# A planned kernel on one core: DMAs put in the program's order, and the planner's durations remade

## The chip, the cores and the metric

The kernel runs on one core of a Trainium2 chip. The core has a matrix engine (TensorE, PE in the profile), a vector engine (VectorE, DVE), a scalar engine (ScalarE, ACT), GpSimd (POOL), and SyncE (SP), which here issues every DMA; 16 DMA engines carry out the transfers. Each engine takes its instructions in a fixed order from a queue of its own and waits at a semaphore where an operand is not there yet. The metric is the device time of one execution in microseconds (us). The kernel before takes 1733.99 us, the median of three runs (1732.49 to 1739.18).

## The reference

One inference step of a trunk of two layers, on a prompt of 1024 tokens and 8 samples of 4 tokens, with D_MODEL = 1024, all in float32. Each layer computes `x + gate(c) * Branch(RMSNorm(x) * (1 + scale(c)) + shift(c))`. Layer 0 is attention in a sliding window of 128 with a sink for each head; layer 1 is a gated DeltaNet with 16 value heads in 8 groups. Its core, cut to what matters:

```python
lower = where(strict, einsum('nbhik,nbhjk->nbhij', kb, kc) * decay, 0.0)
sol = triangular_solve(lower + eye(chunk), rhs, lower=True, unit_diagonal=True)
w_v, w_k = sol[..., :dv], sol[..., dv:]
def step(S, xs):
    u = w_v_c - einsum('bhck,bhkv->bhcv', w_k_c, S)
    o = einsum('bhck,bhkv->bhcv', q_dec_c, S) + einsum('bhij,bhjv->bhiv', qk_c, u)
    S = S * g_tot_c + einsum('bhck,bhcv->bhkv', k_dec_c, u)
    return S, o
out = (rms_norm(o, o_norm_g) * silu(z)) @ w_out
```

The outputs are the rows of the prompt and the samples after a last norm, the new caches of keys and values, the convolution states, and the DeltaNet states of prompt and samples. The states of the samples are 8 x 16 matrices of 128 x 128, 8 MB read and 8 MB written.

## The kernel before

A product in float32 is made of three matmuls: both operands are split into a high part and a rest (`wh` and `wl`, `h2hi` and `h2lo`), and high·high, rest·high and high·rest are summed. The prompt is cut into 8 blocks of 128 tokens; a projection takes one 128-column tile of weights against all 1056 rows in three groups of 384, 384 and 288 columns (`project`, `ps_pj`). These projection matmuls are the filler: everything else is put between them.

Who comes when is decided while the program is written. `Engine` wraps each engine of the core, so that every instruction goes through `Core.issued`. It keeps a clock for each engine (`free`), and for each tile when it was last written and used (`written`, `used`); it adds the duration of the instruction from a small table and links it to the one before on its engine with an edge "program order". Work beside the projections is written as generators that `weave` puts in a list of jobs by rank (`K`, `KR`). After each projection matmul `stages` lets each job go on as long as its condition holds: `ready`, `soon` and `idle` compare the planner's clocks with TensorE's, `bank` waits for a free PSUM bank, `until` runs the jobs until something has come about. So the durations decide how many projection matmuls are laid between, say, a product and the instruction that needs its result. Every recorded instruction has line L89 in the profile (the wrapper's call).

DMA issues were not linked before: they have a place by their data dependences, and the library's scheduler put them into SP's queue.

The parts that the texts below speak of:
- `solve(hq)` makes the products of the keys of head group `hq` (`cst,kT` are transposes, `kT,kT` the products) and scales them into `UZ`; `invert(hq)` inverts 64 triangular 32x32 blocks at once in 31 steps on VectorE, each a product into `tmp` and a subtraction from `X`, 62 rows in all; `diagonal` and `blocks` put these into the whole inverse (`Xd,UZ` products, a transpose of `Xd` into `UZ` on VectorE, `UZ,M` products).
- `decayed(hq)` scales the `qT,kT` products into `DP` on VectorE, `chain(hq)` is the recurrence over 8 chunks. Ahead of the key projection of the group after next the program waits until the chain is finished (`until(lambda: finished[0] >= r - 1)`), so the end of `chain(0)` has no projections beside it.
- The convolution (`conv`) of each projection tile runs as nine `qT`, `kT` or `vT` rows on VectorE (three taps for each of three column groups).
- `out_block(b)` is the output projection of block `b`: it loads `of<-gTd`, adds to the row block `xt<-x2d` and stores `out_y_p<-xt`, with two buffers of `xt`. Beside it `new_states` renews the samples' states: it loads a unit into a buffer (`S<-in_state_gdn_s`), scales it and adds a product (`U,kb`), and stores it (`out_new_s_s<-S`); there are three buffers, and each turn of its loop first fetches the unit two ahead and at its end stores its own. From some point on a unit is 8 heads, 512 KB.

Of the kernel before, what the change touches and what calls it, by code (L numbers as in the profile page):

```python
# [5 lines left out]
F32 = mybir.dt.float32  # L6
# [71 lines left out]

class Engine:
# [16 lines left out]
class Core:  # L96


    def __init__(self, tc):
        self.tc, self.nc = tc, tc.nc  # L100
        self.free, self.last = {}, {}
        self.written, self.used, self.slots, self.parts, self.wide = {}, {}, {}, set(), {}
        self.group = 0
# [7 lines left out]
    def issued(self, eng, op, ins, args, kwargs):  # L111
        aps = [a for a in (*args, *kwargs.values()) if hasattr(a, "tensor")]
        outs = [a for a in (kwargs.get("out", aps[0]), kwargs.get("accum_out")) if a is not None]
        srcs = [a for a in aps if not any(a is o for o in outs)]
        n = 1
        for d in outs[0].shape[1:]:
            n *= d
        start = self.free[eng]
        for a in srcs:
            start = max(start, self.after(self.written, a, eng))  # L120
            if a.space == PSUM:
                start = max(start, self.after(self.used, a, eng))
        for a in outs:
            if self.used.get(self.key(a), (0.0, ""))[1] != "sync" or eng != "sync":
                start = max(start, self.after(self.used, a, eng))
        if "dma" in op:
            self.free[eng] = start + 0.45
            end = start + 2.4
        else:
            rate, fixed = {"tensor": (2400 if op == "matmul" and srcs[0].dtype == F32R  # L130
                                      else 1200 if op == "transpose" else 600, 0.004),
                           "scalar": (1200, 0.06 if op == "copy" and srcs[0].space == PSUM else 0.14
                                      if srcs and srcs[0].space == PSUM else 0.18),
                           "vector": (960, 0.13 if op == "scalar_tensor_tensor" else 0.08),
                           "gpsimd": (420, 0.02 if n >= 256 else 0.14)}[eng]
            if op == "matmul" and outs[0].shape[0] <= 64 and srcs[0].dtype == F32:
                rate = 2400 if n <= 64 and outs[0].shape[0] <= 32 else 600 * P / outs[0].shape[0] if self.group != outs[0].offset // outs[0].ap[0][0] else rate
            if eng == "tensor":
                self.group = outs[0].offset // outs[0].ap[0][0]
            if op == "tensor_scalar_mul" and srcs and srcs[0].space != PSUM and eng == "vector":  # L140
                rate = 1920
            if op == "memset":
                rate = 1e9
            end = self.free[eng] = start + fixed + n / rate
            if eng in self.last:
                self.tc.add_manual_dep(ins, self.last[eng],
                                       mybir.DependencyInfo(mybir.DependencyClass.NoSync, mybir.DependencyReason.DATA),
                                       reason="program order")
            self.last[eng] = ins.name
        for a in srcs:  # L150
            self.used[self.key(a)] = max(self.used.get(self.key(a), (0.0, "")), (end, eng))
        for a in outs:
            self.written[self.key(a)] = self.used[self.key(a)] = (end, eng)

    def key(self, a):

        if a.tensor.name in self.wide:
            return a.tensor.name, a.offset % a.ap[0][0] // self.wide[a.tensor.name]
        return (a.tensor.name, a.offset) if a.tensor.name in self.parts else a.tensor.name

    def after(self, table, a, eng):
        t, e = table.get(self.key(a), (0.0, eng))
        return t + (0.0 if e == eng == "tensor" else 0.1 if e == eng else 0.2)

    def slot(self, key, bufs, t):
# [3 lines left out]
        if len(q) > bufs:  # L169
            self.used[q[-1]] = self.used.get(q[-1 - bufs], (0.0, ""))  # L170
# [7 lines left out]
class Watched:  # L178
# [3 lines left out]
    def tile(self, shape, dt, tag=None, name=None, bufs=None):  # L182
# [5 lines left out]
        self.core.used.setdefault(t.tensor.name, (self.since, "pool"))  # L188
# [31 lines left out]
def body(tc, I, O, cst_ap, dbg=None):  # L220
# [316 lines left out]
    def bank(tag):  # L537
# [5 lines left out]
        yield lambda: plain() or nc.after(nc.used, t, "tensor") <= nc.free["tensor"]  # L543
# [220 lines left out]
    if True:  # L764
# [38 lines left out]
        def kproj(pr):  # L803
# [10 lines left out]
            def evac(gi, a0, b0, pj):  # L814
                if pr == 1 and gi == 0:
                    until(lambda: begun[0] >= 2 * NB)
                    zo[1] = zp.tile([P, 4, T], F32, tag="zo1", name="zo")
                    nc.parts.add(zo[1].tensor.name)
# [217 lines left out]
        def cached():  # L1036

            nonlocal sa_guard, sa
            yield lambda: attended[0] == 4 * NB
# [134 lines left out]
        def open_wo(n):  # L1174
# [3 lines left out]
            for w, nm in ((whi, "whi"), (wlo, "wlo")):  # L1178
                t_ = wo.tile([P, n, D], F32R, name=nm)
                nc.parts.add(t_.tensor.name)  # L1180
# [110 lines left out]
        nc.parts.add(zo[0].tensor.name)  # L1291
# [21 lines left out]
    if True:  # L1313
# [10 lines left out]
        nc.parts.add(x1d.tensor.name)  # L1324
# [320 lines left out]
    if True:  # L1645
# [7 lines left out]
        for XR in XRs:  # L1653
            nc.wide[XR.tensor.name] = GW
            nc.gpsimd.memset(XR[:, 0:3], 0.0)
# [449 lines left out]
        def place_out(k0, wh_, wl_):  # L2105

            nc.parts |= {wh_.tensor.name, wl_.tensor.name}
# [85 lines left out]
        nc.parts |= {x2d.tensor.name, gTd.tensor.name}  # L2193
# [525 lines left out]
```

## Time and profile before

| | |
|---|---|
| median of three runs | 1733.99 us |
| profiled execution | 1732.34 us |
| span of its instructions | 1730.6 us |
| PE busy | 1621.2 us, 94%, 10666 matmuls |
| DVE busy | 1174.6 us, 68%, 3538 |
| ACT busy | 862.6 us, 50%, 2514 |
| POOL busy | 675.5 us, 39%, 1576 |
| mean granted clock of TensorE | 0.98 |
| DMA | 191.82 MB, 111 GB/s over the span |

The profile is of one execution. A row of a timeline gives the start and the length of an instruction (or of a run of like ones, with their count), its engine and line, output and inputs, and in brackets how long the engine stood idle before it and what it waited for. A row of the view of waits gives the engine and its output, what it waited for, the total, the number and the longest. A row of the view of windows gives a stretch of time and the busy time of each engine in it, then the granted clock, the share of DMA time and the rate in GB/s. SPq is SP's queue of DMA issues. The ends of matmuls are modelled: rows of one engine may overlap, and the distance from start to start is the time that one takes.

### The profile page before, as it was taken

The page shows a single profiled execution, that of the slowest core. Times are in us where ns is not written, and L with a number is a line of the kernel's source. Part 1 is how long each engine was busy: PE and PEld are TensorE (multiplying, and loading weights), DVE is VectorE, ACT ScalarE, POOL GpSimd, SP SyncE. Part 2 cuts the span into 40 slices and gives each one's busy share as a digit, 9 for nine tenths or more (in the row PEclk, how much of TensorE's full clock was granted, in tenths as well). Part 3 has the DMA queues.
Part 4 walks back from the last instruction along what each step waited for, and adds up shares of the span by engine and source line. Part 5 has one row for each costly group of instructions (what it writes and reads, how often), then busy time and mean ns, then how long its engine had stood idle before and what let it go on. Part 6 is the DMA issues. An engine that isn't in the chain of part 4 may idle for free. (4 is left out here: it accounts for less than half of the span.)

```text
span 1730.6 us, 32224 instructions
## 1 busy us (share of the span) xinstructions
PE 1621.2 (94%) x10666; PEld 1429.5 (83%) x10666; DVE 1174.6 (68%) x3538; ACT 862.6 (50%) x2514; POOL 675.5 (39%) x1576
## 2 busy tenths in 40 slices
PE   6999999999999999589999999999999998989897
PEld 5987888977788889469989999899999996657675
DVE  4426675555565787757878778778697776357676
ACT  5625555453335664166554655554655655332332
POOL 2601121122213356235544654546356565323332
PEclk9999999999999999799999999999999999999998
DMA  9542122234233323122412324224132237764885
GB/s 330 153 133 73 51 58 55 51 103 114 92 122 97 105 55 85 29 68 69 127 42 73 102 58 114 65 69 117 46 104 70 56 93 227 218 190 138 244 268 171
DMA packets 281577, 191.82 MB, mean 111 GB/s; under 512 B 98361, under 2 KB 253881, under 8 KB 281378
## 3 DMA queue, kind: packets, MB, share of 16 engines
q1 hardware_dynamic: 281410, 189.75, 38.2%
q8 instruction: 85, 1.39, 0.3%
q14 instruction: 82, 0.67, 0.1%
HBM read 144.68 MB, written 47.04 MB: 111 GB/s over the span
## 5 line engine op out<-in xcount | busy, mean ns | idle before, releaser
L89 POOL TENSOR_TENSOR wl<-wr,wh 128x128 fp32r<-128x128 f32 x488 | 236.7, 515 | 485.5 <-ACT wh L89 449.4
L89 PE MATMUL ps_pj<-h2hi,wh 128*128 128x384 f32 (+1 forms) x1128 | 379.9, 337 | 0.0
L89 PE MATMUL ps_pj<-h2lo,wh 128*128 128x384 f32 (+1 forms) x1128 | 378.1, 335 | 0.0
L89 PE MATMUL ps_pj<-h2hi,wl 128*128 128x384 f32 (+1 forms) x1128 | 376.8, 334 | 0.0
L89 PEld LDWEIGHTS ps_pj<-h2hi,wh 128*128 128x128 f32 x1128 | 213.2, 189 | 3.1 <-ACT wh L89 0.2
L89 PEld LDWEIGHTS ps_pj<-h2hi,wl 128*128 128x128 f32 x1128 | 213.2, 189 | 2.7 <-POOL wl L89 0.2
L89 PEld LDWEIGHTS ps_pj<-h2lo,wh 128*128 128x128 f32 x1128 | 213.0, 189 | 2.2
L89 POOL TENSOR_TENSOR xt<-xt,y 128x512 f32<-128x512 f32 (+1 forms) x48 | 63.6, 1328 | 194.3 <-DVE y L89 170.4
L89 PE MATMUL ps_pj<-hlo,wh 128*128 128x384 f32 (+1 forms) x360 | 119.1, 331 | 0.0
L89 PE MATMUL ps_pj<-hhi,wh 128*128 128x384 f32 (+1 forms) x360 | 118.4, 329 | 0.0
L89 PE MATMUL ps_pj<-hhi,wl 128*128 128x384 f32 (+1 forms) x360 | 118.1, 328 | 0.0
L89 DVE SCALAR_TENSOR_TENSOR vT<-XR,cT,vT 128x384 f32<-128x384 f32 (+1 forms) x144 | 83.9, 591 | 47.4 <-ACT vT L89 45.3
L89 DVE TENSOR_TENSOR tmp<-X 64x31 f32<-64x31 f32 (+15 forms) x248 | 89.0, 359 | 16.9 <-POOL X L89 13.4
L89 DVE TENSOR_TENSOR X<-X,tmp 64x31 f32<-64x31 f32 (+15 forms) x248 | 90.7, 366 | 8.5
L89 ACT CAST wh<-wr 128x512 fp32r<-128x512 f32 x122 | 75.1, 617 | 16.4 <-PE ps_pj L89 11.3
L89 POOL TENSOR_TENSOR Xd<-Xc,cst 32x128 f32<-32x128 f32 x128 | 62.7, 490 | 40.5 <-DVE UZ L89 24.4
L89 PEld LDWEIGHTS ps_pj<-hlo,wh 128*128 128x128 f32 x360 | 67.7, 188 | 10.5 <-issue 10.5
L89 ACT COPY XR<-ps_pj 128x384 f32<-128x384 f32 (+1 forms) x96 | 43.0, 448 | 59.5 <-PE ps_pj L89 59.4
L89 PEld LDWEIGHTS ps_pj<-hhi,wh 128*128 128x128 f32 x360 | 67.7, 188 | 4.0 <-issue 3.1
L89 ACT ACTIVATE prob<-prob,nm 128x256 f32<-128x256 f32 (+1 forms) x128 | 62.2, 489 | 15.5 <-DVE nm L89 15.3
L89 PEld LDWEIGHTS ps_pj<-hhi,wl 128*128 128x128 f32 x360 | 67.7, 188 | 2.2 <-issue 2.1
L89 ACT ACTIVATE qe<-ps_mi,Eg 128x128 f32<-128x128 f32 x112 | 34.9, 363 | 60.4 <-PE ps_mi L89 60.3
(574 smaller groups left out, 4203.9 us busy)
## 6 DMA issues: line engine op xcount, KB each, us to landing
wr<-in_gdn_w_in SPq DMA_DIRECT2D x96, 256.0 KB
S<-in_state_gdn_s SPq DMA_DIRECT2D x40, 256.0 KB
xt<-in_x_prompt SPq DMA_DIRECT2D x16, 512.0 KB
wm<-in_w_mod SPq DMA_DIRECT2D x16, 512.0 KB
wr<-in_swa_w_in SPq DMA_DIRECT2D x64, 128.0 KB
wmod<-in_w_mod SPq DMA_DIRECT2D x32, 256.0 KB
wm<-in_w_mod SPq DMA_DIRECT2D x32, 256.0 KB
DP<-gcr SPq DMA_DIRECT2D x64, 128.0 KB
```

The source lines that it names most:

```text
L89: inst = fn(*args, **kwargs)
```

## The change

Five things change, all in the planner. (1) The edge "program order" is added behind every instruction, DMA issues included, so that SP's queue has the order in which the program wrote them. (2) Durations are taken by engine, operation, shape and operands (`on_tensor`, `on_scalar`, `on_vector`, `on_gpsimd`), with TensorE at half speed for 4 us after a gap of more than 2.2 us, table loads on ScalarE, waits between VectorE and GpSimd for a shared port, and a queue of transfers. (3) Tiles are tracked by the box of rows and columns that an access touches (`box`, `note`, `over`) in place of the whole tile or of a listed part (`parts`, `wide`). (4) The latencies between engines are new (`after`), and the time at which a buffer is free comes from `freed`, which leaves out uses by the same engine. (5) `bank` asks `freed`, and the stage `cached` also waits until the stage `modulate` is over. The ranks and all that is computed stay.

```diff
@@ Core.issued
-            if self.used.get(self.key(a), (0.0, ""))[1] != "sync" or eng != "sync":
-                start = max(start, self.after(self.used, a, eng))
+            start = max(start, self.freed(a, eng))
         if "dma" in op:
-            self.free[eng] = start + 0.45
-            end = start + 2.4
+            self.free[eng] = start + 0.48
+            onto = outs[0].space != DRAM
+            size = outs[0].shape[0] * n if onto else int(np.prod(outs[0].shape))
+            part = min(4 * self.run(outs[0]), 4 * self.run(srcs[0]), 4096)
+            work = size * 4 / part * (8.5 + part * 0.0375) * 7e-5
+            self.queue = max(self.queue, start + 0.9) + work
+            few = (outs[0] if onto else srcs[0]).shape[0] <= 64 and part >= 2048
+            end = done = max(start + 2.0, self.queue + 1.0 + work * (1.5 if few else 0.5))
         else:
-            rate, fixed = {"tensor": (2400 if op == "matmul" and srcs[0].dtype == F32R
...
-            end = self.free[eng] = start + fixed + n / rate
-            if eng in self.last:
-                self.tc.add_manual_dep(ins, self.last[eng],
...
+            start, dur, late = getattr(self, "on_" + eng)(op, start, base, n, outs, srcs, args, kwargs)
+            self.free[eng], end, done = start + dur, start + dur + late, start + dur + 0.02
+        if eng in self.last:
+            self.tc.add_manual_dep(ins, self.last[eng],
...
     def after(self, table, a, eng):
-        t, e = table.get(self.key(a), (0.0, eng))
-        return t + (0.0 if e == eng == "tensor" else 0.1 if e == eng else 0.2)
+        lag = {"tensor": 0.054, "gpsimd": 0.078}.get(eng, 0.036)
+        return max((t + (0.06 if e == "sync" else 0.02 if e == eng else lag) for t, e in self.over(table, a)
+                    if not e == eng == "tensor"), default=0.0)
+
+    def freed(self, a, eng):
+        lag = {"tensor": 0.054, "gpsimd": 0.078}.get(eng, 0.036)
+        return max((t + lag for t, e in self.over(self.used, a, a.space == PSUM) if e != eng), default=0.0)
+
+    def on_tensor(self, op, start, base, n, outs, srcs, args, kwargs):
+        if start - base > 2.2:
+            self.slow = 4.0
+        rows = outs[0].shape[0]
+        tiled = rows <= 64 and srcs[0].dtype == F32 and op == "matmul"
...
+        elif srcs[0].dtype == F32R:
+            dur = max(0.108, n / 2400 + 0.014)
+        else:
+            dur = (1 if op == "transpose" else 2) * max(0.108, n / 1200 + 0.003)
...
@@ bank
-        yield lambda: plain() or nc.after(nc.used, t, "tensor") <= nc.free["tensor"]
+        yield lambda: plain() or nc.freed(t, "tensor") <= nc.free["tensor"]
@@ cached
-            yield lambda: attended[0] == 4 * NB
+            yield lambda: attended[0] == 4 * NB and over("modulate")()
```

Where this moves instructions: first VectorE's queue at the end of the inverse of head group 0 and the start of that of group 1 (`X` and `tmp` are rows of the inverse, `qT` rows are convolution taps, `DP` rows scale the products of `decayed`, and the transpose puts a diagonal block into `UZ`). Before:

```order
L89 SCALAR_TENSOR_TENSOR qT<-XR_6117,cT,qT 128x256
L89 TENSOR_TENSOR tmp<-X 64x60
L89 TENSOR_TENSOR X<-X,tmp 64x2x30
L89 SCALAR_TENSOR_TENSOR qT<-XR_6117,cT,qT 128x256
L89 TENSOR_TENSOR tmp<-X 64x31
L89 TENSOR_TENSOR X<-X,tmp 64x31
L89 TENSOR_SCALAR epq<-gsq 128x8
L89 SCALAR_TENSOR_TENSOR DP<-ps_lg,sj,DP 128x128 x14
L89 TENSOR_TENSOR tmp<-X 64x31
L89 TENSOR_TENSOR X<-X,tmp 64x31
L89 STREAM_TRANSPOSE UZ<-Xd_6600 128x512
```

And of the change:

```order
L92 TENSOR_TENSOR tmp<-X 64x31
L92 TENSOR_TENSOR X<-X,tmp 64x31
L92 SCALAR_TENSOR_TENSOR qT<-XR_6141,cT,qT 128x384 x3
L92 SCALAR_TENSOR_TENSOR qT<-XR_6141,cT,qT 128x256 x3
L92 TENSOR_SCALAR epq<-gsq 128x8
L92 SCALAR_TENSOR_TENSOR DP<-ps_lg,sj,DP 128x128 x7
L92 STREAM_TRANSPOSE UZ<-Xd_6579 128x512
L92 SCALAR_TENSOR_TENSOR DP<-ps_lg,sj,DP 128x128
L92 COPY UZ<-ps_lg 32x4x32
L92 SCALAR_TENSOR_TENSOR DP<-ps_lg,sj,DP 128x128 x3
L92 TENSOR_TENSOR tmp<-X 64x31
L92 TENSOR_TENSOR X<-X,tmp 64x31
```

The inverse of group 0 ends ahead of six of the nine `qT` rows in place of behind all of them, and the first transpose stands ahead of the inverse of group 1, in place of behind its first step. The second transpose comes behind all 62 rows of that inverse in both, here with five more `DP` rows ahead of it:

```order
L92 TENSOR_TENSOR tmp<-X 64x31
L92 TENSOR_TENSOR X<-X,tmp 64x31
L92 SCALAR_TENSOR_TENSOR DP<-ps_lg,sj,DP 128x128 x5
L92 STREAM_TRANSPOSE UZ<-Xd_6581 128x512
L92 STREAM_TRANSPOSE UZ<-Xd_6579 128x512
```

On TensorE, between the first `Xd,UZ` products and the `UZ,M` products of 64 columns that need the second transpose, there are 59 projection matmuls before (35 of 384 columns and 24 of 288) and 111 in the change (63 and 48), with a group of `qT,kT`. The change has its first rows of that place so:

```order
L92 MATMUL ps_lg<-Xd_6579,UZ 128x96 x4
L92 MATMUL ps_pj<-h2hi,wh 128x384
L92 MATMUL ps_pj<-h2lo,wh 128x384
L92 MATMUL ps_pj<-h2hi,wl 128x384
L92 MATMUL ps_pj<-h2hi,wh 128x384
L92 MATMUL ps_pj<-h2lo,wh 128x384
L92 MATMUL ps_lg<-UZ,M 32x32 x4
L92 MATMUL ps_lg<-qT,kT 128x128 x4
```

Before, `UZ,M` of 32 columns came 60 rows behind the first `Xd,UZ`, right behind the second group of them; the `qT,kT` products lay ahead of both.

Then SP's queue in the last stage (`S` are state buffers, the number is that of the tile). Before:

```order
L89 DMA out_new_s_s<-S_19891 128x8x128
L89 DMA out_y_p<-xt 128x1024
L89 DMA S_20034<-in_state_gdn_s 128x8x128
L89 DMA out_new_s_s<-S_19918 128x8x128
L89 DMA xt<-x2d 128x1024
L89 DMA of<-gTd 128x4x128
L89 DMA S_20098<-in_state_gdn_s 128x8x128
L89 DMA of<-gTd 128x4x128
L89 DMA out_y_p<-xt 128x1024
L89 DMA out_new_s_s<-S_19940 128x8x128
```

And of the change:

```order
L92 DMA out_new_s_s<-S_19890 128x8x128
L92 DMA S_20078<-in_state_gdn_s 128x8x128
L92 DMA of<-gTd 128x4x128
L92 DMA out_new_s_s<-S_19947 128x8x128
L92 DMA S_20127<-in_state_gdn_s 128x8x128
L92 DMA out_y_p<-xt 128x1024
L92 DMA xt<-x2d 128x1024
L92 DMA of<-gTd 128x4x128
L92 DMA out_new_s_s<-S_20035 128x8x128
L92 DMA S_20221<-in_state_gdn_s 128x8x128
L92 DMA of<-gTd 128x4x128
```

A store and the load into the buffer that it empties stand next to each other in the change, nine times for `S` and five for `xt` between the first state load of 512 KB and the last state store; before, another issue stands between them in most cases.

More of the change, by code (lines that the diff above doesn't have):

```diff
@@ new lines, in on_vector @@
+    def on_vector(self, op, start, base, n, outs, srcs, args, kwargs):
+        scaled = op.startswith("tensor_scalar")
+        rate = 1920 if scaled and (not srcs or srcs[0].space != PSUM) else 960
+        fixed = 0.075
+        if op == "scalar_tensor_tensor":
+            fixed = 0.128 if n > 32 else 0.09
+        elif scaled and len(srcs) > 1:
+            fixed = 0.13
+        elif op == "transpose":
+            fixed = 0.1
+        dur = 0.0 if op == "memset" else fixed + n / rate
+        big = sum(a.space != PSUM and np.prod(a.shape[1:]) >= max(2, n // 2) for a in srcs)
+        if big > 1 or big and rate == 1920:
+            for x, y in reversed(self.pool[-12:]):
+                if x <= start < y:
+                    start = y
+            self.port.append((start, start + dur))
+        return start, dur, 0.08
```

138 lines of the change are left out of this document (97 added, 41 removed).

## The prediction

> **What bounds the kernel now.** I read the windows first, one per stage: start; attention layer; projections and first head group of the DeltaNet layer; its first recurrence, `chain(0)`; the seven later head groups; the output projection with the sample states; and the end of that.
>
> ```profile
> core 0: us, PE busy (x) PEld busy (x) DVE busy (x) ACT busy (x) POOL busy (x), PEclk, DMA share, GB/s
> 0.00:43.00 43.00, 28.98 (x215) 23.20 (x216) 20.86 (x77) 21.79 (x36) 10.50 (x22) 0.96 0.98 331
> 43.00:389.00 346.00, 338.76 (x2367) 296.24 (x2367) 193.99 (x696) 183.46 (x563) 81.68 (x152) 1.00 0.30 84
> 389.00:692.00 303.00, 290.82 (x1814) 254.72 (x1812) 196.19 (x579) 143.49 (x363) 110.89 (x222) 0.99 0.34 96
> 692.00:779.00 87.00, 60.21 (x460) 48.99 (x461) 59.53 (x164) 32.94 (x105) 26.47 (x86) 0.86 0.20 49
> 779.00:1428.00 649.00, 634.97 (x4444) 603.74 (x4444) 511.89 (x1467) 377.12 (x1199) 345.32 (x970) 1.00 0.30 80
> 1428.00:1600.00 172.00, 156.27 (x877) 115.55 (x877) 101.04 (x266) 63.35 (x158) 62.96 (x99) 0.96 0.65 193
> 1600.00:1731.00 131.00, 111.16 (x497) 87.09 (x494) 91.09 (x293) 40.44 (x93) 37.70 (x29) 0.95 0.75 228
> ```
>
> The rows sum to PE 1621 busy of 1731. Length less PE busy gives the idle time: 14.0, 7.2, 12.2, 26.8, 14.0, 15.7 and 19.8, together 109.8 us. TensorE is the bound, and its work stays: the change can only move idle time and the clock. VectorE comes near it only in `chain(0)` (59.5 against 60.2). So I read what ended the idle time, and where the last matmul stands.
>
> ```profile
> PE ps_lg L89 <- DVE UZ L89: 19.0, 6, 16.9
> PE ps_pj L652 <- DVE dg L640: 11.7, 2, 9.8
> PE ps_mi L89 <- ACT kb L89: 6.8, 4, 3.3
> PE ps_tr L89 <- ACT vT L89: 5.6, 5, 2.3
> PE ps_lg L89 <- DMA S<-in_state_gdn_s: 5.3, 3, 2.3
> PE ps_lg L89 <- DVE KQT L89: 4.4, 1, 4.4
> ...
> PE ps_lg L89 <- ACT kT L89: 3.6, 2, 3.3
> ...
> 1717.84 0.39 PE L89 MATMUL ps_ob<-h2lo,ohi 128*128 128x512 f32 x1
> ```
>
> (Total us, times, longest.) Of the 109.8, the 14.0 at the start (most of it the 11.7 behind `dg`) stand in an order that the change leaves alone, and 1730.6 − 1718.2 = 12.4 is the tail behind the last matmul: 109.8 − 14.0 − 12.4 = **83 us** are open to the change. One wait is large, 16.9; the rest are many of 1 to 4 us.
>
> **The change, part by part.** Nothing is computed differently: no term for added or removed work. The sum goes by stage against the profiled execution, 1732.34 us (span 1730.6), which is 1.65 below the median of 1733.99.
>
> *The long wait in `chain(0)`.*
>
> ```profile
> 678.79 1.03 PE L89 MATMUL ps_lg<-Xd,UZ 128*128 128x96 f32 x8
> ...
> 689.05 1.03 PE L89 MATMUL ps_lg<-Xd,UZ 128*128 128x96 f32 x8
> 690.65 0.44 PE L89 MATMUL ps_lg<-UZ,M 128*32 128x32 f32 x8 [0.58 <-ACT M L89]
> 708.01 1.06 PE L89 MATMUL ps_lg<-UZ,M 128*32 128x64 f32 x16 [16.92 <-DVE UZ L89]
> ...
> 680.86 0.18 DVE L89 TENSOR_TENSOR tmp<-X 64x31 f32<-64x31 f32 x1 [2.00 <-POOL X L89]
> ...
> 681.20 0.69 DVE L89 STREAM_TRANSPOSE UZ<-Xd 128x512 f32<-128x512 f32 x1
> ...
> 706.42 0.60 DVE L89 SCALAR_TENSOR_TENSOR DP<-ps_lg,sj,DP 128x128 f32<-128x128 f32 x2
> 706.94 0.69 DVE L89 STREAM_TRANSPOSE UZ<-Xd 128x512 f32<-128x512 f32 x1
> ```
>
> VectorE takes the second transpose of `UZ` only behind the whole triangular inverse of the next head group (680.86 to 706.4, 25.6 us). In the changed order the second transpose still stands behind all 62 rows of that inverse: the wait stays. What changes is TensorE's cover. Between the first `Xd,UZ` and the waiting `UZ,M` (of 64 columns) TensorE now has 59 projection matmuls (35 of 384 columns, 24 of 288), which fill 679.8 to 689.05: 9.2 us, 0.157 each. Changed it has 111 (63 and 48): 111 × 0.157 = 17.4, and four `qT,kT` products, about 1 like the group of `Xd,UZ`: 9 us more cover. Against it, seven more `DP` rows of 0.3 and a small copy stand between the two transposes, 2.3 us. So 16.9 − 9.2 + 2.3 = 10 remain: **−7**. Bounds: −16.9 (all covered) to +2.3 (the cover then lacks elsewhere in `chain(0)`, which has no projections of its own). That the inverse of the first group starts and ends earlier in the new order is how the cover grows (the first diagonal product comes earlier in TensorE's row); it is not counted again.
>
> After long waits the clock is lower. Behind those of 3.27 and 16.92 us:
>
> ```profile
> 628.56 0.47 PE L89 MATMUL ps_lg<-cst,kT 128*128 128x128 f32 x1 [3.27 <-ACT kT L89]
> ...
> 709.00:715.00 6.00, 5.49 (x42) 4.73 (x42) 2.67 (x6) 0.49 (x1) 2.43 (x6) 0.50 0.28 44
> 628.00:634.00 6.00, 5.44 (x31) 5.44 (x32) 5.57 (x14) 5.01 (x18) 0.98 (x2) 0.72 0.03 5
> ```
>
> Of the six microseconds behind each, 6 × 0.28 = 1.7 and 6 × 0.50 = 3.0 are lost. The first is counted with the small waits; the second stays as long as ten microseconds of its wait do.
>
> *The small waits, 43 to 692.* 7.2 + 12.2 = 19.4 idle, and 1.7 of clock. The planner thought an operand ready there and it wasn't (`kT`, `vT`). With durations and latencies nearer to the traces a matmul is put later, behind filler that exists here in plenty (TensorE is at 0.97). Bounds: all gone, with the clock, −21; or a third more of them, +7, since another order makes new ones. Nearest is what is left in the best stage, 43 to 389, which idles at 2.1%; 389 to 692 at that rate would keep 6.4 of its 12.2 and lose 5.8: **−6**.
>
> *779 to 1428:* 14.0 idle in 649, already 2.2%. By the same bounds −14 to +5; I take **−4**, most of what `vT` makes. *1428 to 1600:* 15.7, with 4.4 behind `KQT` and 5.3 behind state loads, which are true chains; the rest is 6: **−4**, bounds −10 to +5.
>
> *The end, 1600 on.* Here transfers decide. SP issues every DMA in one row, and an issue that waits holds all behind it.
>
> ```profile
> SPq L89 <- DMA out_new_s_s<-S: 31.9, 12, 7.0
> SPq L89 <- DMA out_y_p<-xt: 20.1, 6, 5.9
> ...
> 1653.22 0.57 SPq L89 DMA_DIRECT2D out_new_s_s<-S  x1
> 1660.04 0.37 SPq L89 DMA_DIRECT2D S<-in_state_gdn_s  x1
> ...
> 1712.96 0.34 SPq L89 DMA_DIRECT2D out_y_p<-xt  x1
> 1716.20 0.33 SPq L89 DMA_DIRECT2D xt<-x2d  x1
> ...
> 1700.37 0.39 PE L89 MATMUL ps_pj<-whB,ohi 128*64 128x512 f32 x1
> 1700.60 0.28 PE L89 MATMUL ps_mi<-U,kb 96*128 96x256 f32 x1
> 1700.72 0.39 PE L89 MATMUL ps_pj<-wlB,ohi 128*64 128x512 f32 x1
> ```
>
> A load into a buffer that was just stored waits for the store to land: 3.24 us with the queue free (1712.96 to 1716.20), 6.8 under load (1653.22 to 1660.04). The new order has each such load right behind its store: 9 pairs of state buffers and 5 of `xt` from the first 512 KB state load to the last state store. The planner's new `freed` skips users on the same engine, so it thinks these 14 waits free. At w us each, and some 13 us for about 30 issues of 0.33 to 0.57, the row takes 14w + 13: 58 us at 3.2, 76 at 4.5, 108 at 6.8. In the same stretch TensorE has (rows of the changed order, 221 matmuls of 512 columns at 0.23, start to start, and 48 state products at 0.12) 57 us, and 128 such matmuls, 29 us, behind the last state product. With only one or two transfers in flight at a time I expect the landing nearer to 3.2 than to 6.8: w = 4.5, so SP is 76 − 57 = 19 late, of which the 29 us behind cover about 10 (they need `of` tiles from the same queue): **+9**. Bounds: −7 (the 6.8 behind `kb` goes, nothing new) to +35.
>
> A rule speaks against this order. The Trainium skill, page "DMA: Bandwidth & Descriptors", section "Anatomy of one DMA — SWDGE (gpsimd) path", says "DMA engines do not wait on semaphores": a wait stands on the issuing sequencer, before dispatch. The rows at 1653.22 and 1660.04 agree, with nothing issued between. Its fit for transfers that GpSimd issues, 2.0 us and one more for each 436 KB, makes 3.2 us of these 512 KB stores (an estimate from that page); the free pair agrees with 3.24, the loaded one does not.
>
> *Sum:* 1732.3 − 7 − 6 − 4 − 4 + 9 = **1720**.
>
> **The rivals.** *The stores land fast.* With w = 3.2, as in the free pair, the row takes 58 against TensorE's 57, and the end costs nothing: 1732 − 21 = **1711**. For it: a row that waits issues less, so the stores meet less traffic. Against: 0.75 DMA share over the last window. By the fit of the Trainium skill's page "DMA: Bandwidth & Descriptors" (section "Anatomy of one DMA — SWDGE (gpsimd) path") w is 3.2 for every such store, so this would be its time, an estimate; the loaded pair of 6.8 speaks against it.
>
> *All waits planned away.* The 83 us less what is true chain (10 in `chain(0)`, 10 at state loads and `KQT`) and what stays at 1% of 1621, 16: 83 − 36 = 47, of which two thirds: 1732 − 32 = **1700**. For it: every listed wait is one that a planner with the right durations could fill. Against: the 16.9 wait comes from the place of one VectorE row, behind the inverse, and that place stays.
>
> *Nothing that binds moves.* The order is dense (0.98 in the long stages); waits that go in one place come back in another, and the end gives up what the middle gains: **1731**. For it: 2.1% idle is left where filler is richest.
>
> *SP holds the end, slower.* In the row of issues w is 6.2 or more, as under load in the trace of before. Then the row takes 14 × 6.2 + 13 = 100, which is 43 beyond TensorE's 57; less 10 that the matmuls behind cover, +33. With half of the gains ahead of it (−10): 1732 + 33 − 10 = **1755**. Each microsecond of w is 14 of the end: with all other gains (21) the change is a loss from w = 5.4 on (14 × 5.4 + 13 − 57 − 10 = 22), with half of them from 4.6. For it: the 31.9 and 20.1 us that SP waits for stores already, and the 0.75 DMA share of the last window. Against: before, state units move every 7 us with TensorE busy, and the pairs were often adjacent there too.
>
> *The change doesn't do what it says.* Not here: the rows of SP in the changed order follow the program, and no row of TensorE goes missing. Its chance lies in the second rival.
>
> **How the numbers follow.** Forecast 1720: 0.30. Stores land fast, 1711: 0.14. All planned away, 1700: 0.11. Nothing binds, 1731: 0.25. SP holds the end, 1755: 0.20. 0.5% of the median is about what a measurement of this kernel can tell: faster means below 1725.3, slower above 1742.7. Faster: 0.11 + 0.14, and 0.27 of the forecast's 0.30 (its own bounds reach past 1725) = 0.52. Same: the other 0.03 and 0.23 of "nothing binds" = 0.26. Slower: 0.20 + 0.02 = 0.22. The range leaves out the outer half of 1700's and of 1755's chance, 0.16: 1700 to 1752. The forecast's own range is 1710 to 1730.
>
> **What would show it.** Right: the wait for `UZ` in `chain(0)` shrinks to about 10 but stays, behind the same inverse; 389 to 692 idles under 7; after 1600 SP's waits for `out_new_s_s` and `out_y_p` rise from 52 to about 14 × 4.5 = 63, and TensorE waits for `of` or `S`, not `kb`. Wrong: the `UZ` wait as long as before (the cover was counted wrongly), SP's waits after 1600 under 40 (the pairs cost nothing: then about 1711), or above 85 (then the third rival). A longer wait for a weight tile anywhere between 43 and 1428 would show that the queue in program order holds loads back, which this sum takes as nothing, since DMA is at 0.30 to 0.34 there and loads are issued two tiles ahead.

## The result and the profile after

The changed kernel takes 1813.67 us (median of 4, 1811.87 to 1816.71) against 1736.59 for the kernel before: 1.0448 of its time, 95% interval 1.0418 to 1.0478. The forecast was 1720, the range 1700 to 1752: wrong by 94 us, on the other side. The stages of the changed kernel, cut at the same projection matmuls as those of before (in the order start of attention to the end; columns as above):

```profile
core 0: us, PE busy (x) PEld busy (x) DVE busy (x) ACT busy (x) POOL busy (x), PEclk, DMA share, GB/s
43.00:389.00 346.00, 341.38 (x2399) 299.10 (x2400) 196.36 (x704) 184.44 (x567) 84.44 (x154) 1.00 0.30 85
389.00:693.00 304.00, 291.13 (x1781) 253.88 (x1780) 197.69 (x586) 141.44 (x360) 113.76 (x220) 0.99 0.32 94
693.00:774.00 81.00, 61.69 (x467) 51.23 (x467) 52.76 (x151) 34.28 (x112) 27.79 (x91) 0.87 0.22 61
774.00:1463.00 689.00, 658.43 (x4548) 608.35 (x4547) 516.15 (x1484) 379.65 (x1193) 344.57 (x970) 1.00 0.28 75
1463.00:1623.00 160.00, 143.50 (x730) 103.06 (x729) 83.32 (x220) 60.28 (x150) 56.30 (x88) 0.96 0.66 198
1623.00:1798.00 175.00, 135.93 (x535) 101.47 (x534) 97.32 (x308) 41.74 (x94) 39.67 (x30) 0.88 0.59 176
```

Two stages grew. The seven later head groups take 689 us in place of 649, with 30.6 of TensorE idle in place of 14.0 (length less busy), and busy time itself is 23 more. Some 8 of these 23 are no loss of time: the stretch holds 104 more matmuls, nearly all `UZ,M` and `Xd,UZ` products, which the kernel before runs in the stage behind (838 matmuls there, 730 in the changed kernel; rows with `UZ` are busy for 82.0 here in place of 73.6). What makes the other 15 was not taken apart. `chain(0)` is 6 shorter. The end takes 175 in place of 128, at a granted clock of 0.88; the same stretch of the kernel before, which the prediction cut elsewhere:

```profile
1590.00:1718.00 128.00, 119.72 (x536) 93.08 (x534) 92.61 (x295) 41.23 (x94) 39.49 (x30) 0.99 0.76 228
```

Where the time went is finer to see by counting. Both kernels run the same 6048 matmuls on split operands (first operand `h2hi`, `h2lo`, `hhi`, `hlo`, `whi`, `wlo`, `whB` or `wlB`; called projection matmuls here) in nearly the same order, so the start of the n-th of them in each timeline can be compared. In us, each kernel less the one before (the columns behind the second are the runs of the next section):

| n | before, at | changed | no edge on DMAs | edge alone | loads moved | 0.15 us slack | before, +0.1 us |
|---|---|---|---|---|---|---|---|
| 2520 (end of `chain(0)`) | 765 | −8.8 | −8.6 | +4.4 | −11.4 | −4.9 | +23.8 |
| 3240 | 939 | −9.0 | −10.2 | +3.6 | −12.4 | −6.8 | +15.4 |
| 3420 | 986 | +14.6 | +13.0 | +3.9 | +12.1 | −1.1 | +39.9 |
| 4500 | 1261 | +10.9 | +7.4 | +3.9 | +8.2 | −3.4 | +37.0 |
| 5220 | 1452 | +40.0 | +40.7 | +5.1 | +41.4 | +12.5 | +45.5 |
| 5580 (the last stage) | 1590 | +32.9 | +30.4 | +11.6 | +24.4 | −3.0 | +38.3 |
| 5640 | 1607 | +34.7 | +30.7 | +13.0 | +24.9 | +14.4 | +50.9 |
| 5940 | 1691 | +75.9 | +41.4 | +44.2 | +23.7 | +8.6 | +42.8 |

The row for 5580 flatters the run with slack: by then it has run 9 fewer of the other matmuls than the kernel before, by 5640 only one fewer.

The waits of TensorE in the changed kernel, over the whole span (total, times, longest):

```profile
PE ps_mi L92 <- ACT kb L92: 14.2, 4, 6.6
PE ps_tr L92 <- ACT ohi L92: 12.8, 4, 6.5
PE ps_lg L92 <- DVE UZ L92: 12.5, 13, 6.4
...
PE ps_tr L92 <- ACT vT L92: 9.5, 10, 2.3
PE ps_lg L92 <- DMA S<-in_state_gdn_s: 6.4, 6, 2.6
PE ps_mi L92 <- DVE us L92: 6.2, 8, 1.8
PE ps_mi L92 <- DVE S L92: 5.7, 8, 1.8
```

The wait for `UZ` is 6.4 at its longest, no more 16.9. At the top now are `kb` (6.8 before) and `ohi` (on that list for the first time), which ScalarE makes in the last stage, and behind them come many small waits. What held ScalarE, and what held SP, in that stage (waits of both engines' queues, the window of the last stage), and one turn of SP's row:

```profile
ACT ohi L92 <- DMA of<-gTd: 68.0, 11, 12.8
...
SPq L92 <- DMA out_new_s_s<-S: 59.5, 14, 6.4
SPq L92 <- DMA out_y_p<-xt: 29.4, 7, 5.1
...
1705.10 0.50 SPq L92 DMA_DIRECT2D out_new_s_s<-S  x1
1710.39 0.37 SPq L92 DMA_DIRECT2D S<-in_state_gdn_s  x1
1710.86 0.53 SPq L92 DMA_DIRECT2D of<-gTd  x1
1711.44 0.50 SPq L92 DMA_DIRECT2D out_new_s_s<-S  x1
1716.80 0.37 SPq L92 DMA_DIRECT2D S<-in_state_gdn_s  x1
...
1715.52 0.62 ACT L92 CAST ohi<-of 128x512 fp32r<-128x512 f32 x1 [5.55 <-DMA of<-gTd]
1716.04 0.90 ACT L92 ACTIVATE kb<-K,cst 96x256 fp32r<-96x256 f32 x2
```

A store is issued at 1705.10, the load behind it stands until 1710.39: 5.3 us, and again 5.4 from 1711.44. The `of` tile can only be asked for between two such stands. ScalarE waits 5.55 us for it at its `ohi` cast, and `kb`, which needs no DMA at all, stands behind that cast in ScalarE's own row. So one wait on SP holds three engines.

The other loss has this face (the stretch that begins behind n = 3240, in the changed kernel; the whole stretch, and then the projection matmuls in it alone):

```profile
956.90:983.60 26.70, 22.03 (x192) 16.81 (x190) 21.05 (x65) 10.74 (x40) 7.10 (x32) 1.00 0.14 46
...
956.90:983.60 26.70, 0.32 (x4) 0.11 (x2) 0.00 (x0) 0.41 (x1) 1.00 0.14 46
```

For 26.7 us TensorE has no projections at all: `chain(2)`, the third recurrence, was not finished when the program came to the key projection that waits for it, and the rest of the chain ran with little beside it. In the kernel before no such gap is longer than 4 us between 780 and 1428. Why the chain was late stands in VectorE's row. In the changed kernel (`vT` are the last value rows of the group, `tmp` and `X` the first and the last rows of the inverse of the next group, `us` the chain's own first rows):

```profile
911.30 0.78 DVE L92 SCALAR_TENSOR_TENSOR vT<-XR,cT,vT 128x256 f32<-128x256 f32 x1 [0.24 <-ACT vT L92]
912.01 0.17 DVE L92 TENSOR_TENSOR tmp<-X 64x31 f32<-64x31 f32 x1
...
937.82 0.18 DVE L92 TENSOR_TENSOR X<-X,tmp 64x31 f32<-64x31 f32 x1
937.93 0.99 DVE L92 SCALAR_TENSOR_TENSOR vT<-XR,cT,vT 128x256 f32<-128x256 f32 x2
...
941.02 0.61 DVE L92 TENSOR_SCALAR us<-ps_ob,sd 128x128 f32<-128x128 f32 x2 [0.39 <-PE ps_ob L92]
```

And in the kernel before:

```profile
913.51 1.53 DVE L89 SCALAR_TENSOR_TENSOR vT<-XR,cT,vT 128x256 f32<-128x256 f32 x3 [1.44 <-ACT vT L89]
917.25 0.61 DVE L89 TENSOR_SCALAR us<-ps_ob,sd 128x128 f32<-128x128 f32 x2 [2.22 <-PE ps_ob L89]
918.88 0.18 DVE L89 TENSOR_TENSOR tmp<-X 64x31 f32<-64x31 f32 x1 [1.01 <-POOL X L89]
```

All 62 rows of that inverse, 26 us, stand ahead of the last two `vT` rows. The chain needs these (TensorE transposes them at 940.12 and takes the result at 940.37), so its first `us` comes at 941.02. Before, the chain's first `us` comes at 917.25, and the inverse follows with the chain's rows in between. So this loss of 24 us hangs on the place of one inverse in VectorE's row.

### The profile page after: what moved, and what is told of

It reads as the page before. It is cut to its first block, busy times and chain, and to the rows that moved or that the text cites. A ratio compares the mean times of both kernels' runs of the same rounds, so it can differ in the third digit from the quotient of the medians.

```text
span 1810.0 us, 32221 instructions
## 1 busy us (share of the span) xinstructions
PE 1660.9 (92%) x10666; PEld 1440.2 (80%) x10666; DVE 1168.4 (65%) x3538; ACT 865.3 (48%) x2514; POOL 680.1 (38%) x1576
## 4 chain that ended last, share of the span: by engine, by line
PE 26%; DMA 8%; DVE 6%; ACT 4%; issue 4%; POOL 3%; SPq 1%; POOLq 0%; ACTq 0%; DVEq 0%
PE ps_pj L92 15%; PE ps_lg L92 4%; PE ps_tr L92 3%; PE ps_mi L92 3%; DMA of<-gTd 2%; PE ps_ob L92 2%; DMA out_new_s_s<-S 2%; POOL rst L92 1%; DVE UZ L92 1%; DMA wr<-in_gdn_w_out 1%; DMA S<-in_state_gdn_s 1%; SPq L92 1%; ACT jk L92 1%; DMA DP<-gcr 1%; DVE DP L92 1%
## 5 line engine op out<-in xcount | busy, mean ns | idle before, releaser
L92 POOL TENSOR_TENSOR wl<-wr,wh 128x128 fp32r<-128x128 f32 x488 | 241.3, 525 | 468.1 <-ACT wh L92 450.6
L92 ACT CAST wh<-wr 128x512 fp32r<-128x512 f32 x122 | 74.7, 614 | 12.4 <-PE ps_pj L92 12.1
L92 PEld LDWEIGHTS ps_pj<-hlo,wh 128*128 128x128 f32 x360 | 67.7, 188 | 10.9 <-issue 10.9
L92 ACT CAST ohi<-of 128x512 fp32r<-128x512 f32 x32 | 19.8, 619 | 104.0 <-DMA of<-gTd 71.5
L92 ACT ACTIVATE prob<-prob,nm 128x256 f32<-128x256 f32 (+1 forms) x128 | 62.3, 489 | 14.6 <-DVE nm L92 14.4
```

The lines of the kernel that those rows point to most:

```text
L92: inst = fn(*args, **kwargs)
```

## The experiments

**First: which part of the change?** Theory A put all of the loss on SP's order, theory B the end alone on it and the middle on the new durations and latencies, theory C all on the durations. Each ratio below is to the kernel before as measured beside that run (medians of 1732.05 to 1735.91). The edge taken from the DMAs:

```diff
-        if eng in self.last:
-            self.tc.add_manual_dep(...)
-        self.last[eng] = ins.name
+        if "dma" not in op:
+            if eng in self.last:
+                self.tc.add_manual_dep(...)
+            self.last[eng] = ins.name
```

> The changed kernel, with the program-order edge taken from the DMA issues again (they are placed by the library's scheduler as before); new durations stay. Measured by the place of the same projection matmuls, the change is 9 us ahead at the first recurrence, loses about 40 in the seven later head groups and about 47 after the first output-projection blocks. If the order of SP's queue makes both losses (theory A), about 1725. If it makes the end alone and the new durations and latencies make the 40 in the middle (theory B), about 1765, with the middle still 35 to 40 behind. If the durations make everything (theory C), 1810.

Measured 1768.65 (1.0202 of before, 1.0171 to 1.0233). The middle is as in the changed kernel to 4 us all along, and the loss of the end falls from 43 (n = 5580 to 5940) to 11. The opposite, the edge alone in the kernel before:

```diff
-            if eng in self.last:
-                self.tc.add_manual_dep(...)
-            self.last[eng] = ins.name
+        if eng in self.last:
+            self.tc.add_manual_dep(...)
+        self.last[eng] = ins.name
```

> The kernel before, with nothing but the program-order edge put on the DMA issues too; durations, latencies and tile tracking as before. Theory A: all of the loss, 1800 to 1820. Theory B: the loss of the end alone, about 1780, and the middle as before (within 5 us). Theory C: within 5 us of the kernel before.

Measured 1783.67 (1.0280, 1.0248 to 1.0313). It runs 3 to 6 us behind over most of the middle and loses 33 from n = 5580 to 5940. Theory B: the edge is worth 45 us in the changed kernel and 52 alone, the planner's numbers 37 alone, and 52 + 37 = 89 is 7 to 12 more than the 77 to 82 that both cost together.

**What in SP's row?** The two loads written later:

```diff
 def rows_of(b, part, t):
-    yield lambda: stored[0] >= b - 1
+    yield lambda: stored[0] >= b - 1 and pos[0] >= 16 * (b - 1) + 14
 def new_states():
         while units:
-            fetch()
             b, h0, n, st = units.pop(0)
...
+            fetch()
             nc.sync.dma_start(S1[b][:, h0:h0 + n], st)
```

> The changed kernel with two loads of the last stage written later in the program: the fetch of a state unit stands behind the products of the current unit (so the buffer that it fills was stored a whole unit earlier), and the load of xt waits until 14 of the 16 steps of the block before are done. If the pairs of a store and the load into the same buffer in SP's row make the end's loss (the third rival of the prediction), SP's waits for out_new_s_s and out_y_p fall from 89 us to under 30 and the time by about 40, to about 1772; the middle stays. If the end is bound otherwise (by bandwidth or by kb), within 10 us of 1813.

Measured 1761.10 (1.0160, 1.0125 to 1.0195): 52.6 less than the changed kernel, all of it behind n = 5220; from 5580 on the last stage no longer loses. SP's waits in this run:

```profile
SPq L92 <- DMA out_new_s_s<-S: 23.7, 9, 5.9
SPq L92 <- DMA out_y_p<-xt: 14.0, 5, 5.6
```

From 89 to 38 us, not under 30 as expected, but enough: ScalarE waits 15.1 us for `of` in place of 68.0. So the pairs are the cause of the end's loss, and two loads written later take it back with the edge in place. Is it that the planner does not know of the wait?

```diff
-... if e != eng), default=0.0)
+... if e != eng or eng == "sync"), default=0.0)
```

> The changed kernel where freed counts uses by the same engine for SP, so that the planner's clock of SP waits for a store before a load into its buffer. The pairs stay next to each other in SP's row. If the loss of the end comes from the row itself, it stays: 1800 to 1815. If it comes from a planner that thinks the loads early and puts kb and ohi copies too early on ScalarE, 20 to 40 us come back: 1775 to 1795.

Measured 1814.42 (1.0459, 1.0421 to 1.0498). The end is as slow as in the changed kernel (SP waits 52.9 and 25.5 us). What it knows changes nothing: the row is in the program's order whatever the planner's clock says. The middle did move, by about 20 us (−7.5 in place of +14.6 at n = 3420, +19.5 in place of +40.0 at 5220): `chain(2)` begins at 904.79 there, between the first rows of the inverse, and the starved stretch is gone, though no latency changed. That already shows how sensitive the middle is to the planner's numbers.

**Second: why does the middle lose?** Theory D: the new latencies are too short for the chip. Theory F: the ranks were fitted to the old planner, and any other order loses. Two nudges of the kernel before that say nothing about the chip tell these apart, and two of the changed kernel without its edge on DMAs:

```diff
 # e5, before
-        return t + (0.0 if e == eng == "tensor" else 0.1 if e == eng else 0.2)
+        return t + (0.0 if e == eng == "tensor" else 0.12 if e == eng else 0.22)
 # e6, before
-                           "vector": (960, 0.13 if op == "scalar_tensor_tensor" else 0.08),
+                           "vector": (960, 0.14 if op == "scalar_tensor_tensor" else 0.09),
 # e7, after without the edge on DMAs (e8: 0.02; e10: 0.3)
-        return max((t + (0.06 if e == "sync" else 0.02 if e == eng else lag) ...
+        return max((t + (0.06 if e == "sync" else 0.02 if e == eng else lag + 0.15) ...
```

> The kernel before with its latency between engines 0.02 us longer in the planner (0.1 to 0.12 and 0.2 to 0.22), nothing else. If its order is good only because the ranks of the jobs were fitted to exactly this planner (theory F), a nudge that says nothing new about the chip should lose a good part of what the new durations lose: 10 to 40 us, so 1742 to 1772, in the middle stages. If the new durations and latencies are wrong for the chip and the old ones right (theory D), 20 ns change next to nothing: within 6 us of 1732.

> The kernel before with 10 ns more for each VectorE instruction in the planner, nothing else. Theory F: 10 to 40 us slower, with another profile of gains and losses along the program than the 20 ns of latency make. Theory D: within 6 us of 1732.

Measured 1723.68 (0.9930, 0.9902 to 0.9958) and 1725.00 (0.9931, 0.9907 to 0.9956). Both are faster than before, by 11 to 12 us: neither theory foresaw that. Theory F is out as it was put: the order of before is not one that any nudge spoils. That orders matter is not out: two nudges that say nothing about the chip moved the time by 11 to 12 us. In the trace of the first the largest single gain is one wait, `UZ` of `chain(0)`:

```profile
PE ps_lg L89 <- DVE UZ L89: 6.2, 7, 2.2
```

The 16.9 us are gone; this run is 9 ahead at the end of `chain(0)`, 17 by n = 3060 (897 us) and 12 at the end. The wait went by the order of VectorE:

```profile
691.98 0.52 DVE L89 TENSOR_TENSOR X<-X,tmp 64x220 f32<-64x220 f32 x1
692.42 0.69 DVE L89 STREAM_TRANSPOSE UZ<-Xd 128x512 f32<-128x512 f32 x1
693.05 0.52 DVE L89 TENSOR_TENSOR tmp<-X 64x231 f32<-64x231 f32 x1
```

The second transpose stands behind 20 of the 62 rows of the next group's inverse (18 in the run with 10 ns), and no more behind all of them.

> The changed kernel without the edge on DMAs (1768.65 measured), with 0.15 us added to its latency between engines when an operand is read. If the new latencies are too short, so that every matmul arrives a little early and waits (theory D), most of the 37 us come back: 1735 to 1745, and the many waits of 0.15 to 1.2 us on TensorE in the middle stages go. Theory F: another order of the same kind, 1745 to 1785, better or worse by luck.

> The same with only 0.02 us added. Theory D: a seventh of the effect of the 0.15, within 6 us of 1768. Theory F: up to 20 us either way, not in proportion to the 0.15 us.

Measured 1740.53 (1.0026, 1.0002 to 1.0050) and 1770.24 (1.0197, 1.0168 to 1.0226): both as theory D said. With 0.15 us more the starved stretch at 957 is gone (its longest gap between 780 and 1440 is 6.3 us) and the middle idles less:

```profile
774.00:1440.00 666.00, 647.89 (x4503) 607.50 (x4502) 511.29 (x1478) 380.42 (x1199) 357.02 (x976) 0.99 0.29 78
```

18.1 idle in 666, against 27.0 in 689 in the run without the edge. With 0.02 us the starved stretch is gone too (`chain(2)` begins at 919.0, among the rows of the inverse; +6.1 at n = 3420 in place of +13.0), yet the whole is no faster: that run falls back to +29.4 by n = 5220 and is +26.9 at 5640, against +30.7. But theory D cannot be right as it stands, since the trace bears out the new latencies. An instance in the changed kernel:

```profile
1708.93 0.62 ACT L92 CAST ohi<-of 128x512 fp32r<-128x512 f32 x1 [4.57 <-DMA of<-gTd]
...
1709.60 0.49 PE L92 MATMUL ps_pj<-whB,ohi 128*128 128x512 f32 x1 [2.91 <-ACT ohi L92]
```

The cast ends at 1709.55, and the matmul that waited for it starts 0.05 us later; the planner has 0.054. So theory G, an argument so far: exact latencies leave no margin. Its test was more margin in both planners, and the two repairs together:

```diff
 # e9, before
-        return t + (0.0 if e == eng == "tensor" else 0.1 if e == eng else 0.2)
+        return t + (0.0 if e == eng == "tensor" else 0.2 if e == eng else 0.3)
 # e11: e3 and e7 in one, with the edge on DMAs;  e12: e5 and the moved loads of e3
```

> The kernel before with 0.1 us more latency in its planner (0.2 on one engine, 0.3 between two). Theory G (what theory D has become): latencies as the traces show them leave no margin, an instruction laid too early makes TensorE wait, one laid late only gets a few more filler matmuls ahead of it; so more margin helps or costs nothing while filler lasts: 1715 to 1730, like the 20 ns (1723.7). If the old latencies are right and any change is a cost (what theory D said first): 1740 and more.

Measured 1786.79 (1.0306, 1.0273 to 1.0339): a miss for theory G as it was put. Where 20 ns gained 12 us, 100 ns cost 53. The table shows that run lose 24 by the end of `chain(0)` and 25 between n = 3240 and 3420, and there it has a starved stretch too, with no projections from 970 to 1014 (the first row is the stretch, the second its projection matmuls alone):

```profile
970.30:1013.90 43.60, 35.91 (x278) 28.36 (x276) 32.94 (x102) 21.40 (x83) 16.09 (x55) 0.96 0.23 63
...
970.30:1013.90 43.60, 0.33 (x4) 0.17 (x2) 0.00 (x0) 0.41 (x1) 0.96 0.23 63
```

It is `chain(2)` again, and by the same order of VectorE:

```profile
965.93 0.18 DVE L89 TENSOR_TENSOR X<-X,tmp 64x31 f32<-64x31 f32 x1
966.03 0.47 DVE L89 SCALAR_TENSOR_TENSOR vT<-XR,cT,vT 128x256 f32<-128x256 f32 x1
```

The whole inverse stands ahead of the last `vT` row, and the chain begins at 971. The traces of all runs agree on this: in the five where all 62 rows stand ahead of the chain (changed, no edge on DMAs, loads moved, before with 0.1 us, and the run with margin in the tests below) 20 to 25 us are lost from n = 3240 to 3420; in the others at most 10 rows do, and the loss is at most 6.3, but for 15.5 in the run with longer ScalarE numbers below, which has a gap of 13 us elsewhere. So more margin is not what decides this piece: the order appears in the changed planner with none and in the old one with 0.1 us more, and it goes from the changed one with 0.02 us more and with a nudge of SP's clock alone. That exact latencies make a chain wait at each hop is not shown.

> The changed kernel without the edge on DMAs, with 0.30 us added to the latency instead of 0.15 (1740.5) or nothing (1768.65). Theory G: the gain flattens: 1725 to 1745. If the gain of the 0.15 was the luck of an order (theory F), anything from 1745 to 1785.

Measured 1732.97 (0.9995, 0.9973 to 1.0017): the gain flattens, as theory G said it would, and the kernel is level with before.

> The changed kernel with its edge on DMAs, and both repairs: 0.15 us added to the latency and the two loads of the last stage moved (as in the run with loads moved, 1761.1). If the two losses are separate and add up, 1813.67 less 52.6 (loads) less about 28 (latency, 1768.65 to 1740.5): 1733, within 8. If moving the loads already gave what the margin gives, 1755 to 1761.

Measured 1744.89 (1.0067, 1.0043 to 1.0091), 4 above the band. It is 68.8 less than the changed kernel, where the two repairs singly gave 52.6 and 28.1, together 80.7: they add up but for 12.

> The kernel before with 0.02 us more latency (1723.7) and the two loads of the last stage moved; DMAs placed by the library's scheduler. If the pairs cost time there too (SP waits 52 us for its stores), 5 to 10 us less: 1714 to 1719. If TensorE's work covers them there, 1721 to 1726.

Measured 1720.47 (0.9923, 0.9896 to 0.9949): the fastest of all runs, 3 below the run with 20 ns alone, which is inside both intervals. Whether the moved loads help there is not settled.

**Third: margin in the tests, or length of the chains?**

```diff
 # e13, after without the edge on DMAs: Core.ready
-        return max((self.after(self.written, t, "tensor") for t in ts), default=0.0)
+        return max((self.after(self.written, t, "tensor") + 0.15 for t in ts), default=0.0)
 # e14, the same kernel: on_scalar
-        fixed = 0.05 if srcs and srcs[0].space == PSUM else 0.095
+        fixed = 0.18 if srcs and srcs[0].space == PSUM else 0.225
 # e15: e10 with the moved loads of e3
```

> The changed kernel without the edge on DMAs (1768.65), with 0.15 us added where a job's test asks whether its operands are ready, and the planner's clocks left exact. If the missing margin in those tests is the cause (theory G), most of the 28 us that 0.15 us in every latency brought back: 1737 to 1750. If it was the slower clocks of the chains instead (each hop longer, so that chains are begun earlier against the filler), little: 1760 to 1772.

Measured 1750.48 (1.0093, 1.0063 to 1.0123): 18 of the 28 us that 0.15 us in every latency brought, half a microsecond above what theory G gave and far from the other. It gained them with the late `chain(2)` still in it (20 us lost from n = 3240 to 3420).

> The same kernel with 0.13 us more for each ScalarE instruction in the planner, about what the planner of before had more; all other durations and all latencies as changed. Theory H: the shorter hops over ScalarE (most of the waits in the middle end on it: vT, vo, uo, cvo, XR) are the part of the new numbers that costs; then 1738 to 1752. If every hop counts alike, a third of the 28: 1757 to 1765.

Measured 1760.26 (1.0139, 1.0098 to 1.0179): 8 us, a third of the 28, as if every hop counted alike. A single order of 8 us says little, where nudges without a meaning moved the time by 11 and 12.

> The changed kernel with the DMAs placed by the library's scheduler, 0.30 us more latency (1733) and the two loads of the last stage moved. If the moved loads help where the scheduler places the DMAs as they did with the kernel before (1723.7 to 1720.5), 1727 to 1731, still behind the kernel before with 20 ns and the same loads (1720.5).

Measured 1729.76 (0.9974, 0.9951 to 0.9997), in the band. With margin, and with the row of SP repaired or left to the scheduler, the new durations are as good as the old ones, and not better than the old ones with 20 ns.

## Why the prediction was wrong, step by step

- **The wait in `chain(0)`, −7: right.** It stayed, behind the same inverse (675.2 to 701.8), with the 111 projection matmuls as cover, and shrank to 6.4 behind `UZ` and 2.4 behind `Xd`, 8.8 in place of 16.9. Between n = 2460 (686 us, +1.7) and 2520 the changed kernel gains 10.5. What the prediction took as fixed is not: "that place stays" held against the rival that plans all waits away, and in the runs with 20 and 10 ns the transpose moves into the inverse and the wait falls to 2.2 and 2.1.
- **The small waits, −6, −4 and −4: wrong, and the largest miss.** 43 to 692 came out at +1, not −6, and 389 to 693 idles 12.9 where under 7 was forecast. From 765 to 1590 the step was −8 and the measure is +41.7 (−8.8 to +32.9), and the run without the edge shows it to be the planner's alone. The sentence that failed is "With durations and latencies nearer to the traces a matmul is put later, behind filler". The diff showed the opposite for most hops: what the planner adds from the start of a ScalarE row to TensorE, beside the part for the columns, went from 0.18 + 0.2 = 0.38 to 0.095 + 0.1 + 0.054 = 0.25, and from VectorE to TensorE from 0.28 to 0.21; from TensorE to ScalarE it stayed near 0.2. So the planner takes an operand to be ready earlier and puts its reader earlier. I counted the waits that the old numbers left and never asked which way the new ones erred. And I read VectorE's order at `chain(0)` only: at `chain(2)` the new order puts the inverse ahead of the rows that the chain needs, and there the changed kernel falls back 24 us (n = 3240 to 3420), more than half of the 41.7.
- **The end, +9: the mechanism right, the size wrong.** It measures +47 (+32.9 to about +80), of which the run without the edge keeps 9. The pairs are what holds the row (SP waits 14 times for state stores and 7 times for `xt`, 89 us, in the whole stage), but the load that waits issues 5.3 us behind its store, not 4.5. By the prediction's own formula 5.3 makes 14 × 5.3 + 13 − 57 − 10 = 20. Two terms were mis-sized beside w. The 10 of cover did not come: the `of` tiles stand between the pairs, ScalarE stops at the cast of `of` (68.0 us), and `kb` stands behind the cast; without the cover the formula gives 30, and TensorE idles 39.1 in place of 8.3. And the sum has no term for the clock: with one matmul fewer TensorE is busy for 135.9 in place of 119.7, 16 more, at a clock of 0.88 in place of 0.99. SP's 89 us passed the 85 that the prediction had named as the sign of the slow end. "SP holds the end" had been given 0.20 and 1755; by its mechanism it was the case, though with w at 5.3 and not at 6.2, and the edge alone in the kernel before cost 52.
- **The fit of 3.2 us for a 512 KB store** from the Trainium skill (page "DMA: Bandwidth & Descriptors", section "Anatomy of one DMA — SWDGE (gpsimd) path") is for transfers that GpSimd issues and did not hold in this queue: 5.3 and 5.4 in the rows at 1705.10 and 1711.44. The prediction expected little traffic in a row that waits; the DMA engines were busy for 0.83 and 0.87 of these two waits, and for 0.44 of the 3.24 at the end of the kernel before. Its other sentence, that the wait stands on the issuing sequencer, is what the moved loads confirm.
- **"Nothing that binds moves"** and **"all planned away"** were both wrong: what binds moved, to SP at the end and to VectorE's order ahead of a chain in the middle. (Two thirds of the second one's 47 are 31, so its time was 1701.)

Still open: why the loss in the middle grows by another 29 us from n = 4500 to 5220, and why the planner lays that inverse first; no run moves that inverse alone. No run takes back the tracking of tiles by boxes, `freed` or the new condition of `cached` alone, so the middle's loss is shown to be the planner's and not which of its parts makes it. Added latency gives 28 and 36 us back, but whether by margin or by other orders is not settled; the parts of the 28 (18 in the tests, 8 on ScalarE) were measured in separate orders and need not add.

## What to carry to other kernels

Before DMAs are put into the program's order, look for each load into a buffer whose last user is a store on the same queue: write the load one unit later, or everything behind it on that queue, and on the engines that wait for that, stands for the time of a landing. More or less latency in a planner shows its worth only in runs (in two planners here +20 ns was worth 12 us and nothing, +100 ns cost 53, +150 and +300 gave 28 and 36 back). After each such change, look where the longest serial block of an engine, here an inverse of 62 rows, has come to stand against the row that the next chain waits for. When a change replaces estimates, work out for one hop which way the sum moves before arguing that truer numbers make a better order.

## What the runs showed of the hardware that was not expected

A load issued behind the store of its buffer waits 5.3 to 5.4 us for 512 KB although SP issues nothing in between (1705.10 to 1710.39); at the end of the kernel before it was 3.24. The share of DMA time in these stretches is 0.83, 0.87 and 0.44. The first two rows are of the changed kernel, the third of the one before:

```profile
1705.00:1710.40 5.40, 2.31 (x10) 1.33 (x8) 2.88 (x14) 1.03 (x2) 0.72 (x1) 1.00 0.83 244
1711.40:1716.80 5.40, 5.40 (x15) 4.24 (x15) 1.36 (x5) 1.28 (x3) 0.00 (x0) 0.50 0.87 243
1713.00:1716.20 3.20, 3.20 (x16) 2.64 (x15) 2.92 (x7) 0.63 (x2) 0.00 (x0) 1.00 0.44 169
```

Gaps of up to 6.6 us on TensorE brought the granted clock of the last stage from 0.99 (1590 to 1718 before) to 0.88. One of them shows how short a gap does it: TensorE waited 2.91 us ahead of the matmul at 1709.60 and, two matmuls later, 0.79 more, and from 1711.4 to 1716.8, with no idle time, its granted clock was 0.50. And in the row shown, the instruction that waits for another engine starts 0.05 us after that one's row ends (1709.55 to 1709.60).
